# Sink probabilities divided before their transposes, and a reordered start and end, in a two-layer encoder trunk

## The chip, the cores and the metric

The kernel runs on one core of one Trainium2 chip. The metric is the device time of one execution in microseconds (us); lower is better. A core has five engines that run their own instruction streams and wait for each other by semaphores: TensorE (PE, matmuls; PEld is its weight load), VectorE (DVE), ScalarE (ACT), GpSimd (POOL) and SyncE (SP). SP, ACT and POOL also issue DMA transfers.

## The reference

Input is `x` of 256 tokens by 1024 columns, all in float32. Two layers follow; each is

```
x = x + 1/2 * SwiGLU_1(RMSNorm(x))                  # 1024 -> 2816 -> 1024
h = RMSNorm(x)
[qA kA vA qB kB vB] = h @ W_in
oA = windowed attention, 8 query heads on 2 key heads, 64 wide, ALiBi, one sink logit a head
oB = differential attention, 4 heads: softmax1 - lambda * softmax2, then RMSNorm per head
x = x + concat(oA, oB) @ W_out
x = x + 1/2 * SwiGLU_2(RMSNorm(x))
```

and a last RMSNorm gives the output. Of the windowed attention the part that matters here is

```python
m = jnp.maximum(jnp.max(scores, axis=-1, keepdims=True), sink_l)
e = jnp.exp(scores - m)
p = e / (jnp.sum(e, axis=-1, keepdims=True) + jnp.exp(sink_l - m))
out = jnp.einsum('bnkgqj,bnjkd->bnqkgd', p.astype(v.dtype), vb)
```

The sink logit takes part in the denominator only.

## The kernel before

**Precision.** Nearly every product is made from three fp32r products. Each operand is split into a high part (a rounding cast to fp32r) and a low part (the value less the high part); the product is high·high + low·high + high·low. For weights, ACT makes the high part and DVE the low part; `emit_split` (line 207) does both for half of one weight load.

**Weights and their order.** All weights stream once from HBM in loads of up to 1 MB (`specs`, one `Step` each). Six raw buffers hold loads that have landed. `ahead(n)` (line 244) emits, as far as half-load number `n`, the next splits, and with each buffer that comes free the next DMA on SP. How far it goes at each point of the program comes from the table `LEAD` (line 32): an entry is a number of half loads ahead of the load then in use; "start" and "open0" serve the first feed-forward block, "first0", "mid0" and "last0" its later groups, "mix" the attention stage, "close" the end of a block. ACT and DVE run their instructions in the order that comes out of this, so an entry decides what stands in front of what on these engines. PE is kept in program order everywhere. In the attention stage, between lines 1035 and 1157, `kept[0]` is False: there a planner orders the instructions of ACT, DVE and POOL by a timeline of its own, and `urgent()` raises the priority of what is made inside it.

**The feed-forward groups.** Groups 2 to 4 of the first feed-forward block of layer 0, and 1 to 4 of the others, are computed by a scheme of seven products in the place of eight (`by_sevens`, line 743), which adds some weight blocks by accumulating DMAs from POOL and some by DVE.

**The start.** `x` is fetched in quarters of 256 columns: the first by ACT's queue, the others by SP's, between the first pieces of the weights (line 473 on). `grow1`, the first norm's gain, is turned into columns by PE. `keep_busy` runs fp32 matmuls of the identity with itself. Then `take_x(0)` transposes two blocks of x on PE (`Norm.turn`), makes the operand's high part on ACT and its low part on DVE (`Norm.operands`), and the splits of the first gate and up weights are interleaved with that. `first_chunk` (line 603) holds the first six real matmuls. The squares for the norm run on ACT, and the norm's factor `r` is applied after the matmuls.

**The norm's factors in the attention stage.** `Norm.spread` (line 457) makes a 128x256 block with each token's factor down a column: DVE multiplies the identity by the factors (`dg`), one fp32 matmul with a block of ones spreads them.

**The attention stage** (`mix`, line 959). Heads of the windowed attention come in four chunks of two heads. `soft_a` (line 1023) makes a chunk: PE's scores, DVE's bias and minimum, ACT's exponential with its sums, then the sink's exponential `es`, added to the denominators `den_a`. It returns the exponentials not divided. `soft_b` does the same for differential attention. `keys_first_a` and `keys_first_b` transpose the probabilities, eight PE transposes and two copies out of PSUM each. While these run, PE makes the value projection of B (`vsl`). The division of A comes at the end: `ra` is the reciprocal of all denominators, POOL spreads it to a block `rw` of the output's layout, `turn_sums` transposes that with four PE transposes for each pair `cp` of chunks and copies it to `rT`, and DVE multiplies the attention output by it before `split`. The products of B with its values (`osl`) stand between the transposes and these.

**The end.** The last down projection is arranged so that the first 128 tokens finish early; `close` adds and squares, `finish(t)` scales 128 rows by the norm's factor, the left 512 columns on ACT and the right 512 on DVE, and stores each half with one DMA (ACT's queue and SP's).

Of the kernel before, what the change touches and what calls it, by code (L numbers as in the profile page):

```python
# [46 lines left out]
def trunk(ctx: ExitStack, tc: tile.TileContext, x, n1, g1, u1, d1, nm, w_in, sink,  # L47
# [159 lines left out]
    def emit_split(i, j):  # L207
# [132 lines left out]
    class Norm:  # L340
# [14 lines left out]
        def turn(self, j):  # L355
            sl = halves(bank())
            for i in range(2):
# [4 lines left out]
        def operands(self, j, sl, between=None):  # L362
            xs = blk()
            self.xs.append(xs)
            gs = [gcol[:, self.g0 + 2 * j + i:self.g0 + 2 * j + i + 1] for i in range(2)]

            def high(i):
                act.activation(xs[:, i, 0:S], sl[:, i], AF.Identity, scale=gs[i])

            def low(i):  # L370
# [3 lines left out]
            if between is None:  # L374
                high(0)
                high(1)
                low(0)
                low(1)
            else:
                high(0)  # L380
                low(0)
                between()
                high(1)
                low(1)
            self.turned.append((j, sl, gs))
# [87 lines left out]
    def fetch_x(q, j):  # L473
        q.dma_start(xk[:, :, j * 256:(j + 1) * 256], x[0].rearrange("(t p) d -> p t d", p=P)[:, :, j * 256:(j + 1) * 256])
# [9 lines left out]
    for j in (2, 3):  # L484
        fetch_x(sp, j)
# [3 lines left out]
    def keep_busy(n):  # L489
        for _ in range(n):  # L490
            pe.matmul(warm[:, 0:P], lhsT=ident, rhs=ident, start=True, stop=True)

    ones = const.tile([P, P], F32, name="ones")
    pool.memset(ones, 1.0)
# [5 lines left out]
    keep_busy(4)  # L500
    pe.transpose(gsl[:, 0:16], grow1, ident[:16, :16])
    keep_busy(1)
# [100 lines left out]
    def first_chunk(accs, xs, w):  # L603
# [3 lines left out]
        for n, (i, rhs) in enumerate(((0, hi), (0, lo), (1, hi))):  # L607
# [77 lines left out]
    def ffn(norm, aside=None, before=None, final=False, sevens=SEVEN[1]):  # L685
# [152 lines left out]
        for k in (0, 2):  # L838
# [3 lines left out]
            if before is take_x:  # L842
                for step, (kk, i) in enumerate(((k, 0), (k, 1), (k + 1, 0), (k + 1, 1))):
                    if step or k:
                        tokens((gs, us)[i], norm.xs, ws[i], 0, (kk,))
                    else:
                        first_chunk(gs, norm.xs, ws[0])
                    if step == 1:
# [110 lines left out]
    def mix(l, norm, nxt_norm):  # L959
# [63 lines left out]
        def soft_a(c, q):  # L1023
# [6 lines left out]
            dve.tensor_tensor(den, den, es, op=ALU.add)  # L1030
            return e
# [42 lines left out]
        for k0 in (0, 4):  # L1074
            w = weights()
            for k in range(4):
# [28 lines left out]
        ra = tmp("ra", 1, (P, 4, 4))  # L1105
# [192 lines left out]
```

## Time and profile before

| | |
|---|---|
| median of 3 runs | 911.79 us (911.65 to 912.84) |
| the profiled execution | 912.2 us |
| its span, first to last instruction | 910.4 us |
| busy PE / DVE / ACT / POOL | 902.3 / 777.5 / 613.8 / 64.9 us |
| moved by DMA | 200.83 MB |

The span lies inside the profiled execution's time; 1.8 us are around it. A line of the timeline gives the start in us from the span's start, the duration, the engine, the line of the kernel (here nearly always that of the helper on line 62, so tiles tell more), the operation, out<-in by tile names, the shapes and the count; in brackets stands the idle time ahead of it and what ended that. `ps` and `xy` are PSUM tiles, `s` the large work tiles (operands, exponentials, probabilities), `w` a split weight, `raw` a landed load, `q` and `v` the operands of the seven products. SPq, ACTq and POOLq are DMA issues. A line of the groups gives busy time and mean ns of one, then idle time ahead. A line of the waits gives us in total, how often, and the longest.

### The profile page before, as it was taken

What the parts mean: (1) busy time and instruction counts of PE and PEld (TensorE: products, weight loads), DVE (VectorE), ACT (ScalarE), POOL (GpSimd) and SP (SyncE); (2) the same over time, 40 slices, a digit from 0 to 9 for tenths busy, and PEclk for the clock granted to TensorE, in tenths of its full rate; (3) what the DMA queues carried; (4) which work ended last, traced back from release to release, by engine and by line L of the source; (5) the groups of instructions that cost most, each with busy time, mean ns of one, the idle gap of its engine ahead of it and who ended that gap; (6) DMA issues with size and microseconds to landing.
All of it is one profiled execution on the core that took longest, in us unless ns stands there. A gap on an engine that the chain in (4) does not pass through costs nothing.

```text
span 910.4 us, 12060 instructions
## 1 busy us (share of the span) xinstructions
PE 902.3 (99%) x4486; PEld 754.2 (83%) x4486; DVE 777.5 (85%) x1053; ACT 613.8 (67%) x975; POOL 64.9 (7%) x83
## 2 busy tenths in 40 slices
PE   9999999999999999999999999999999999999997
PEld 8888888888888888888888888888888888888886
DVE  5859999879876899999778999997896878999894
ACT  6856677677776766677575776676766686776660
POOL 0411000000001001000000101000001000101011
PEclk9999999999999999999999999999999999999999
DMA  9998897956048788897966898897720786898731
GB/s 331 336 271 235 232 317 249 266 141 224 1 145 236 176 269 247 239 306 249 304 186 163 254 282 265 238 303 214 219 98 1 256 215 176 235 311 250 222 114 47
DMA packets 114060, 200.83 MB, mean 221 GB/s; under 512 B 3663, under 2 KB 31377, under 8 KB 114001
## 3 DMA queue, kind: packets, MB, share of 16 engines
q1 hardware_dynamic: 97344, 167.53, 54.1%
q0 software_dynamic: 16096, 31.75, 20.1%
q8 instruction: 35, 0.57, 0.3%
q10 hardware_dynamic: 560, 0.79, 0.3%
q14 instruction: 25, 0.20, 0.1%
HBM read 199.00 MB, written 1.05 MB: 220 GB/s over the span
## 4 chain that ended last, share of the span: by engine, by line
PE 91%; DMA 5%; DVE 1%; ACT 1%; issue 1%; POOL 0%; SPq 0%; POOLq 0%; ACTq 0%
PE ps L62 69%; PE xy L62 22%; DMA raw<-in_ffn_w_up_dram 4%; DVE w L62 1%; DMA raw<-in_ffn_w_gate_dram 1%; ACT w L62 1%; ACT junk L62 0%; POOL r L62 0%; ACT s L62 0%; DVE s L62 0%; ACT tmp L62 0%; SPq L172 0%; DVE xk L62 0%; DVE q L62 0%; POOLq L1293 0%
## 5 line engine op out<-in xcount | busy, mean ns | idle before, releaser
L62 DVE TENSOR_TENSOR w<-raw,w 128x1024 fp32r<-128x1024 f32 (+1 forms) x458 | 476.7, 1099 | 36.1 <-ACT w L62 35.1
L62 PE MATMUL ps<-w,s 128*128 128x512 f32 (+1 forms) x2046 | 473.7, 389 | 0.3 <-DVE s L62 0.3
L62 ACT CAST w<-raw 128x1024 fp32r<-128x1024 f32 (+1 forms) x458 | 405.0, 953 | 60.6 <-DVE raw L62 40.9
L62 PEld LDWEIGHTS ps<-w,s 128*128 128x128 f32 x2046 | 380.2, 188 | 78.7 <-ACT tmp L62 0.8
L62 PE MATMUL xy<-w,s 128*128 128x512 f32 x528 | 125.7, 391 | 0.0
L62 PEld LDWEIGHTS xy<-w,s 128*128 128x128 f32 x528 | 98.3, 188 | 20.3
L62 PE MATMUL xy<-w,q 128*128 128x512 f32 x360 | 88.1, 393 | 0.0
L62 PEld LDWEIGHTS xy<-w,q 128*128 128x128 f32 x360 | 66.5, 188 | 13.2
L62 PE MATMUL ps<-s,w 128*128 128x512 f32 (+1 forms) x384 | 70.2, 339 | 0.0
L62 POOL DMA_DIRECT2D raw<-in_ffn_w_up_dram x30 | 38.9, 1315 | 432.6 <-DVE w L62 262.6
L62 DVE TENSOR_TENSOR raw<-raw,raw 128x2048 f32<-128x2048 f32 x30 | 68.7, 2289 | 0.5
L62 PEld LDWEIGHTS ps<-s,w 128*128 128x128 f32 x384 | 58.9, 188 | 8.4
L62 ACT ACTIVATE s<-ps,gcol 128x256 fp32r<-128x256 f32 (+1 forms) x80 | 31.4, 478 | 38.3 <-PE ps L62 38.3
L62 PE MATMUL ps<-w,q 128*128 128x512 f32 x180 | 43.2, 389 | 0.0
L62 PE MATMUL ps<-w,v 128*128 128x512 f32 x180 | 43.2, 389 | 0.0
L62 ACT CAST s<-ps 128x512 fp32r<-128x512 f32 x32 | 18.1, 593 | 36.5 <-PE ps L62 36.3
L62 PEld LDWEIGHTS ps<-w,q 128*128 128x128 f32 x180 | 33.8, 188 | 7.0
L62 PEld LDWEIGHTS ps<-w,v 128*128 128x128 f32 x180 | 33.8, 188 | 7.0
L62 DVE TENSOR_TENSOR s<-ps,s 128x512 fp32r<-128x512 f32 x32 | 21.3, 688 | 18.0 <-ACT s L62 17.9
L62 ACT ACTIVATE s<-s,negm 128x256 f32<-128x256 f32 x64 | 31.7, 498 | 6.1 <-DVE negm L62 6.0
L62 PE MATMUL ps<-ident,s 128*128 128x128 f32 x256 | 34.0, 273 | 0.0
L62 PEld LDWEIGHTS ps<-ident,s 128*128 128x128 f32 x256 | 29.7, 140 | 4.8 <-issue 0.8
(128 smaller groups left out, 557.2 us busy)
## 6 DMA issues: line engine op xcount, KB each, us to landing
raw<-in_ffn_w_down_dram SPq DMA_DIRECT2D x44, 1024.0 KB, 7.3
raw<-in_ffn_w_gate_dram SPq DMA_DIRECT2D x39, 1024.0 KB, 7.4
raw<-in_ffn_w_up_dram SPq DMA_DIRECT2D x39, 1024.0 KB, 7.1
raw<-in_ffn_w_up_dram POOLq DMA_DIRECT2D x30, 1024.0 KB, 9.8
raw<-in_w_in_dram SPq DMA_DIRECT2D x14, 1024.0 KB, 7.7
raw<-in_ffn_w_gate_dram SPq DMA_DIRECT2D x8, 512.0 KB, 8.0
raw<-in_ffn_w_up_dram SPq DMA_DIRECT2D x8, 512.0 KB, 9.0
raw<-in_w_in_dram SPq DMA_DIRECT2D x8, 512.0 KB, 6.8
```

The costliest lines, as they stand in the source:

```text
L62: ins = issue(*a, **k)
```

## The change

1. `soft_a` divides each chunk's exponentials by the denominators at once: a reciprocal and a broadcast product on DVE. `ra`, `rw`, `turn_sums` and the product by `rT` go; `split` reads the attention output from PSUM. The order of the transposes changes: `keys_first_b(1)` comes after the value projection, `keys_first_a(2)` and `(3)` after the `osl` products; the scaling of `vB` is made urgent.
2. The first 256 columns of x come as two eighths, on ACT's queue and on SP's; `take_x` turns and splits them one after the other; DVE instead of ACT casts the very first weight piece; `first_chunk` takes its second and third products in the other order. `keep_busy` multiplies a tile `wake` that DVE sets, and has six calls in the place of seven.
3. `spread` gives the factors in a high and a low part by two fp32r matmuls.
4. The last 128 rows are scaled and stored in column quarters, by four DMAs.
5. Entries of `LEAD` change.

```diff
-LEAD = dict(start=(5, 7, 10, 10),
-            open0=(2, 0, 0, 2, 6, 6, 8, 6, 5, 6, 1, 10, 2, 5, 7, 7, 8, 0),
-            first=(1, 1, 1, 7, 12, 15, 16, 19, 19, 22, 22),
+LEAD = dict(start=(2, 7, 8, 6),
+            open0=(2, 0, 0, 2, 3, 6, 8, 6, 5, 6, 1, 10, 1, 5, 7, 6, 8, 0),
+            first=(1, 1, 2, 8, 12, 15, 16, 19, 19, 22, 22),
...
-            mid0=(6, 9, 12, 14, 15, 15, 19, 19, 19, 22, 24),
-            last0=(2, 8, 12, 13, 15, 15, 19, 20, 20, 23, 25),
-            first0=(2, 3, 3, 4, 7, 11, 11, 14, 14, 18, 18),
-            open=(8, 12, 11, 9, 11, 11, 9, 5),
-            close0=(7, 5, 7, 5, 6, 10, 3, 10, 5, 11, 4, 7, 1),
-            close=(1, 8, 9, 9, 6, 8, 8, 9, 1, 7, 5, 4, 6),
-            mix=(10, 2, 0, 2, 9, 2, 3, 5, 6, 11, 5, 2, 3, 1, 6, 5, 2, 4, 1, 6, 7, 8, 6, 11, 7, 8))
+            mid0=(4, 9, 12, 15, 15, 15, 19, 19, 19, 22, 24),
+            last0=(2, 8, 12, 13, 15, 15, 19, 20, 20, 22, 25),
+            first0=(0, 0, 3, 6, 6, 11, 11, 11, 12, 18, 18),
+            open=(10, 11, 9, 7, 11, 11, 9, 5),
+            close0=(6, 3, 7, 5, 6, 10, 3, 10, 5, 11, 4, 6, 1),
+            close=(0, 8, 9, 9, 6, 2, 7, 6, 1, 10, 5, 4, 8),
+            mix=(10, 0, 0, 0, 11, 3, 2, 6, 8, 9, 5, 1, 3, 0, 3, 5, 2, 2, 4, 5, 4, 8, 1, 10, 4, 9))
@@ emit_split
-            act.copy(h_, r_)
+            if i + j + a:
+                act.copy(h_, r_)
+            else:
+                dve.tensor_copy(h_, r_)
+                yield
@@ spread
-            dg = tmp("dg", 1, (P, S))
+            dg = tmp(dt=F32R)
             for t in range(2):
-                dve.tensor_scalar_mul(dg[:, t * P:(t + 1) * P], ident, self.r[:, t:t + 1])
-            pe.matmul(sl[:, 0:S], lhsT=ones, rhs=dg, start=True, stop=True)
+                c, r = slice(t * P, (t + 1) * P), self.r[:, t:t + 1]
+                dve.tensor_scalar_mul(dg[:, 0, c], ident, r)
+                dve.scalar_tensor_tensor(dg[:, 1, c], in0=ident, scalar=r, in1=f(dg[:, 0, c]), op0=ALU.mult, op1=ALU.subtract)
+            for i in range(2):
+                pe.matmul(sl[:, 0:S], lhsT=ones, rhs=dg[:, i], start=i == 0, stop=i == 1)
@@ the start
-    fetch_x(act, 0)
+    fetch_x(act, 0, P)
+    wake = const.tile([P, P], F32, name="wake")
+    dve.memset(wake, 1.0)
...
+        if j == 0:
+            fetch_x(sp, P, P)
         if j == 1:
-            fetch_x(sp, 1)
+            fetch_x(sp, 256)
@@ take_x
         if k == 0:
-            sl = norm.turn(0)
-            keep_busy(2)
+            norm.sl = norm.turn(0, (0,))
+            keep_busy(1)
             next(g)
-            norm.operands(0, sl, lambda: next(u))
+            norm.operands(0, norm.sl, (0,))
+            next(g)
+            next(u)
+        elif k == 0.25:
+            norm.operands(0, norm.turn(0, (1,), norm.sl), (1,))
             next(g)
             next(u)
@@ soft_a
             dve.tensor_tensor(den, den, es, op=ALU.add)
+            dve.reciprocal(es, den)
+            ev = e.rearrange("p t (a n) -> p (t a) n", a=2)
+            dve.tensor_tensor(ev, ev, es.unsqueeze(2).to_broadcast([P, 4, 256]), op=ALU.mult)
             return e
@@ mix
-                    aT.append(keys_first_b(1))
+        with urgent():
+            act.activation(vB[:, 0], vsl[0], AF.Copy, scale=norm.r[:, 0:1])
+            dve.tensor_scalar_mul(vB[:, 1], vsl[1], norm.r[:, 1:2])
+        aT.append(keys_first_b(1))
         pT = [keys_first_a(0)]
-        act.activation(vB[:, 0], vsl[0], AF.Copy, scale=norm.r[:, 0:1])
-        dve.tensor_scalar_mul(vB[:, 1], vsl[1], norm.r[:, 1:2])
-        for c in range(1, 4):
-            pT.append(keys_first_a(c))
+        pT.append(keys_first_a(1))
...
+        for c in (2, 3):
+            pT.append(keys_first_a(c))
@@ the products with the values
-            rT = turn_sums(cp)
...
-            dve.tensor_tensor(t_, oa[cp], rT, op=ALU.mult)
-            split(oT[cp], t_)
+            split(oT[cp], oa[cp])
@@ finish
-        act.mul(ob[:, 0], xk[:, t, 0:512], rf)
-        dve.scalar_tensor_tensor(ob[:, 1], in0=xk[:, t, 512:D], scalar=rf, in1=gf[0][:, 1], op0=ALU.mult, op1=ALU.mult)
-        for j, q in enumerate((act, sp)):
-            q.dma_start(out[0, t * P:(t + 1) * P, j * 512:(j + 1) * 512], ob[:, j])
+        for c in ((0, 512),) if t == 0 else ((0, 256), (256, 512)):
+            a, b = [slice(j * 512 + c[0], j * 512 + c[1]) for j in range(2)]
+            oa, og = ob[:, 0, c[0]:c[1]], ob[:, 1, c[0]:c[1]]
+            act.mul(oa, xk[:, t, a], rf)
+            dve.scalar_tensor_tensor(og, in0=xk[:, t, b], scalar=rf, in1=gf[0][:, 1, c[0]:c[1]], op0=ALU.mult, op1=ALU.mult)
+            sp.dma_start(out[0, t * P:(t + 1) * P, b], og)
+            (sp if t and c[0] == 0 else act).dma_start(out[0, t * P:(t + 1) * P, a], oa)
```

More of the change, by code (lines that the diff above doesn't have):

```diff
@@ L353, in pair, with turn @@
             self.operands(j, self.turn(j))
-        def turn(self, j):
-            sl = halves(bank())
-            for i in range(2):
+        def turn(self, j, of=range(2), sl=None):
+            sl = halves(bank()) if sl is None else sl
+            for i in of:
                 for t in range(2):
@@ L360, in turn, with operands @@
             return sl
-        def operands(self, j, sl, between=None):
-            xs = blk()
-            self.xs.append(xs)
+        def operands(self, j, sl, of=range(2)):
+            if 0 in of:
+                self.xs.append(blk())
+            xs = self.xs[j]
             gs = [gcol[:, self.g0 + 2 * j + i:self.g0 + 2 * j + i + 1] for i in range(2)]
-            def high(i):
+            for i in of:
                 act.activation(xs[:, i, 0:S], sl[:, i], AF.Identity, scale=gs[i])
-            def low(i):
+            for i in of:
                 dve.scalar_tensor_tensor(xs[:, i, S:512], in0=sl[:, i], scalar=gs[i], in1=f(xs[:, i, 0:S]),
                                          op0=ALU.mult, op1=ALU.subtract)
[L374 to L385, printed above, removed]
+            if 1 in of:
+                self.turned.append((j, sl, gs))
         def copies(self, n=KC // 2):
@@ L490, in keep_busy @@
         for _ in range(n):
-            pe.matmul(warm[:, 0:P], lhsT=ident, rhs=ident, start=True, stop=True)
-    ones = const.tile([P, P], F32, name="ones")
-    pool.memset(ones, 1.0)
+            pe.matmul(warm[:, 0:P], lhsT=wake, rhs=wake, start=True, stop=True)
+    ones = const.tile([P, P], F32R, name="ones")
+    pool.memset(f(ones), 1.0)
     mhalf = const.tile([P, 8], F32, name="mhalf")
@@ L847, in ffn @@
                         first_chunk(gs, norm.xs, ws[0])
+                        before(0.25)
                     if step == 1:
@@ L1102, in turned @@
             return halves(sl)
-        ra = tmp("ra", 1, (P, 4, 4))
-        dve.reciprocal(ra, den_a)
-        rw = blk(F32)
-        for t in range(2):
-            pool.tensor_copy(rw[:, t].rearrange("p (c a d) -> p c a d", c=4, a=2),
-                             ra[:, :, 2 * t:2 * t + 2].unsqueeze(3).to_broadcast([P, 4, 2, 64]))
-        def turn_sums(cp):
-            turned(rw, cp, rsl[cp])
-            rT = tmp()
-            act.copy(rT, halves(rsl[cp]))
-            return rT
         oT = [blk() for _ in range(4)]
-        rsl, both = [bank() for _ in range(2)], pair()
+        both = pair()
         osl = both
```

14 lines of the change are left out of this document (6 added, 8 removed).

## The prediction

> **What bounds the kernel now.** I read the page first, then who waited for whom on the TensorE, then stretches, then the order of time at the places that the change touches.
>
> ```profile
> span 910.4 us, 12060 instructions
> PE 902.3 (99%) x4486; PEld 754.2 (83%) x4486; DVE 777.5 (85%) x1053; ACT 613.8 (67%) x975; POOL 64.9 (7%) x83
> ```
> ```profile
> PE ps L62 <- DVE s L62: 0.3, 1, 0.3
> ```
> ```profile
> 25.00:50.00 25.00, 25.00 (x116) 20.81 (x115) 22.09 (x25) 20.16 (x30) 11.57 (x31) 1.00 1.04 339
> 70.00:190.00 120.00, 120.00 (x556) 99.82 (x556) 112.69 (x124) 82.21 (x111) 5.14 (x4) 1.00 0.89 259
> 239.40:246.20 6.80, 6.80 (x52) 5.79 (x52) 4.77 (x24) 5.19 (x21) 0.00 (x0) 1.00 0.01 2
> 246.20:253.20 7.00, 7.00 (x65) 7.00 (x64) 4.23 (x7) 3.16 (x6) 1.16 (x2) 1.00 0.00 1
> ```
>
> The third fence gives a stretch in us from the span's start and its length, then the busy time of PE, weight loads, DVE, ACT and POOL, the granted TensorE clock, the DMA share and GB/s. PE (TensorE) is busy 99% of the span, its clock is granted in full (1.00 in each stretch), and behind its first matmul its list of waits has one entry, 0.3 us. A modelled busy time can hide stalls, so I also looked at the distances between matmul starts. So the time is: when the first real matmul starts, plus the PE work, plus what follows the last matmul. An edit can gain only where it removes PE work, starts it sooner or shortens the tail; anything on DVE (VectorE) or ACT (ScalarE) gains nothing by itself and loses where PE comes to wait. DVE is the next bound, 112.69 of 120 us in the stretch from 70 to 190. The DMA engines are full early (share 1.04 from 25 to 50).
>
> **The change, part by part.**
>
> *Sink division.* Each mixing stage now turns a spread-out block of reciprocals with eight PE transposes (`turn_sums`, four for each `cp`). They go, with POOL's spreading copies, two ACT copies, two DVE products and the reciprocal `ra`.
>
> ```profile
> 239.35 0.26 DVE L62 TENSOR_TENSOR den_a<-den_a,es 128x4 f32<-128x4 f32 x2 [1.18 <-ACT es L62]
> 240.50 0.48 DVE L62 CUSTOM_DVE_ANT_0 s<-ps,distA,nsnk 128x256 f32<-128x256 f32 x1 [0.89 <-PE ps L62]
> 245.46 0.28 ACT L62 ACTIVATE es<-es 128x4 f32<-128x4 f32 x2
> 246.16 3.65 PE L62 MATMUL ps<-ident,s 128*128 128x128 f32 x32
> 249.65 3.74 PE L62 MATMUL xy<-v,s 128*128 128x128 f32 x32
> 253.22 0.60 PE L62 MATMUL ps<-ident,s 128*128 128x128 f32 x4
> 253.75 1.95 PE L62 MATMUL ps<-s,vA 128*64 128x256 f32 x16
> 255.63 0.66 PE L62 MATMUL ps<-ident,s 128*128 128x128 f32 x4
> 256.22 1.95 PE L62 MATMUL ps<-s,vA 128*64 128x256 f32 x16
> ```
> ```profile
> 253.39 31.29 PE ps L62 x164
> 700.53 31.29 PE ps L62 x164
> ```
>
> From start to start the two groups hold PE for 253.75 - 253.22 = 0.53 and 256.22 - 255.63 = 0.59 us: 1.12 us a layer. The chain has the same piece of 31.29 us in both layers, so 2 x 1.12 = **-2.2 us**. That is on the path, since PE is. The transposes of the probabilities stay, only in another order (`keys_first_b(1)` later, `keys_first_a(2)` and `(3)` behind the 32 `osl` matmuls).
>
> What comes in is on DVE: for each of four chunks a reciprocal and a 128x1024 product whose second operand is a broadcast.
>
> ```profile
> L62 DVE TENSOR_TENSOR w<-raw,w 128x1024 fp32r<-128x1024 f32 x354 | 411.6, 1220 | 31.0 <-ACT w L62 30.1
> L62 DVE COPY s<-ps 128x512 f32<-128x512 f32 x12 | 8.3, 689 | 1.3 <-PE ps L62 1.1
> L62 DVE SCALAR_TENSOR_TENSOR s<-s,rc 128x256 f32<-128x256 f32 x16 | 7.0, 479 | 0.1
> L62 DVE RECIPROCAL rc<-den_b 128x2 f32<-128x2 f32 x8 | 1.3, 159 | 0.6 <-ACT s L62 0.6
> L62 DVE CAST distA<-dist_i 128x512 f32<-128x512 int32 x1 | 0.4, 417 | 0.0
> ```
>
> No such broadcast product is in the trace. A subtraction of that size took 1.220 us; I take that (four of the 256-wide form would be 4 x 0.479 = 1.9, the upper end; two of the 512-wide cast 0.8, the lower). So 4 x (1.22 + 0.16) = 5.5 us a layer, ahead of the transposes. From 239.4 to 253.2 DVE is idle 13.8 - 4.77 - 4.23 = 4.8 us. It nearly fits. Followed through: the first two products can run from 239.9, when their sums are there (239.35 + 0.26, two reciprocals; DVE idled until 240.50), to about 242.4. The other two need sums whose `es` was made at 245.46; the scores ahead of them now wait 1.9 us for DVE (242.4 instead of 240.5), so these products end near 251. PE transposes at (249.65 - 246.16) / 32 = 0.109 us. The eight of `keys_first_b(1)` are gone from their earlier place, so it comes to 246.16 - 0.87, does 24 there (2.62), then `osl` (253.22 - 249.65 = 3.57), and wants chunk 2 at 251.5 and chunk 3 at 252.4. A lucky order makes the wait 0, a copy or two (0.69) in front of the last product about 1 us a layer. I take 0.25: **+0.5 us** in all. Waiting behind these products on DVE stand PSUM copies of the transposes (0.69 each) and `vB`, which the change marks urgent; they have that same slack. The later `split(oT, oa)` reads PSUM directly: shorter, and hidden behind the output projection.
>
> *Spread in two parts.* One fp32 matmul becomes two fp32r ones of 256 columns.
>
> ```profile
> 193.52 1.55 PE L62 MATMUL xy<-s,w 128*128 128x512 f32 x8
> 197.68 0.59 PE L62 MATMUL ps<-dg,ones 128*128 128x256 f32 x2
> 197.92 0.93 PE L62 MATMUL ps<-s,w 128*128 128x512 f32 x3
> ```
>
> The old one appears as two instructions and the next starts 197.92 - 197.68 = 0.24 us later, which looks like no gain. But the three after it (512, 256 and 512 wide) take 0.93, where the eight of the row above (four of each width) take 1.55, so (1.55 - 0.28) / 7 = 0.18 a matmul, and three should take 0.35 + 0.39 = 0.74. The 0.19 us missing belongs to the old spread: 0.43. Two fp32r matmuls of 256 columns cost about 0.23. So -0.2 twice, **-0.4 us**. (The Trainium skill, "FP8 and Floating Point Precision", section TensorE Precision Notes, says true fp32 takes four passes through the array. The 0.43 agrees with four passes better than the 0.24 does; by the bare 0.24 this term would be 0.) Its two more DVE instructions (under 0.48 each) lie between 193.8 and 195.8, where DVE waits for PE.
>
> *First eighth of x, DVE cast, earlier warm-up, the new order.*
>
> ```profile
> 3.07 0.49 SPq L474 DMA_DIRECT2D xk<-in_x_dram  x1
> 4.49 0.62 ACT L62 CAST w<-raw 128x512 fp32r<-128x512 f32 x1 [1.77 <-DMA raw<-in_ffn_w_gate_dram]
> 5.27 0.47 ACT L62 ACTIVATE s<-ps,gcol 128x256 fp32r<-128x256 f32 x1 [0.16 <-PE ps L62]
> 5.79 1.83 PE L62 MATMUL ps<-w,s 128*128 128x512 f32 x6
> 8.83 0.60 PE L62 MATMUL ps<-ident,xk 128*128 128x128 f32 x4
> ```
> ```profile
> xk<-in_x_dram SPq DMA_DIRECT2D x1, 256.0 KB, 5.3
> ```
>
> Today ACT casts the weights from 4.49 and only then makes the operand (5.27 + 0.47), so PE starts at 5.79. With the cast on DVE (0.42 to 0.69, by the rows above) both can be ready at 5.0 to 5.2: 0.6 to 0.8 us sooner. But PE next needs the second quarter of x, which lands at 3.07 + 5.3 = 8.4 and is transposed at 8.83; sooner than 8.4 to 8.6 it cannot go on. One more DMA on SP ahead of it (0.49 of issue) moves no bytes ahead, yet could push it by 0.5. So -0.4 to 0; I take **-0.2 us**. `wake` only lets `keep_busy` begin before the identity is there; whatever it speeds up in the first matmuls ends at the same landing, so it adds 0.
>
> *The planner's lists.* At 69 us stands the only stall of the body:
>
> ```profile
> 65.66 3.49 DVE L62 TENSOR_TENSOR w<-raw,w 128x1024 fp32r<-128x1024 f32 x3
> 69.07 0.68 DVE L62 TENSOR_TENSOR s<-ps,s 128x512 fp32r<-128x512 f32 x1
> 69.16 0.39 PE L62 MATMUL ps<-w,s 128*128 128x512 f32 x1
> 69.81 2.56 PE L62 MATMUL ps<-w,s 128*128 128x512 f32 x10 [0.26 <-DVE s L62]
> ```
>
> 69.81 - 69.16 = 0.65 between starts where 2.56 - 0.39 over nine steps gives 0.24: 0.4 us lost, because `turn_one`'s subtraction stands behind three weight subtractions. The new `first0` begins (0, 0, 3) instead of (2, 3, 3): fewer weights ahead of it. That takes **-0.4 us** if the weights themselves still come in time. In the opening the lists ask for less ahead (start 2 instead of 5):
>
> ```profile
> 17.65 1.14 ACT L62 CAST w<-raw 128x512 fp32r<-128x512 f32 x2
> 18.41 5.60 PE L62 MATMUL ps<-w,s 128*128 128x512 f32 x24
> ```
>
> This cast moves behind the squares, to end near 21.2, and PE wants it half way through the 24 matmuls, at 18.41 + 2.7 = 21.1: a tie. What the other changed entries do can't be read off; each moves half a load, one DVE subtraction of 1.22 us, and I put them at 0: nothing below (no other stall is there to remove), and some single subtractions, 1 to 5 us, above.
>
> *Last rows in four DMAs.*
>
> ```profile
> 905.60 0.75 DVE L62 SCALAR_TENSOR_TENSOR s<-xk,rf,s 128x512 f32<-128x512 f32 x1 [0.67 <-POOL rf L62]
> 906.36 0.36 ACTq L62 DMA_DIRECT2D out_dram<-s  x1
> ```
>
> Halves are ready at 905.60 + 0.48 = 906.1 and 906.5, but SP issues three of the four, 0.36 each: 906.1, 906.4, 906.8. The last is issued 0.4 us later than now and carries half the bytes, worth 128 KB at 339 GB/s = 0.4. I take **0**, between -0.4 and +0.4. (The Trainium skill, "DMA: Bandwidth & Descriptors", section Anatomy of one DMA, gives about 2.0 us fixed and the rest by bytes: as an estimate from that page half the bytes land 0.3 us sooner, and the term would be +0.1. No run here shows a transfer of that half size.)
>
> **Sum.** -2.2 + 0.5 - 0.4 - 0.2 - 0.4 + 0 = -2.7 us. The profiled execution took 912.2 (span 910.4 and 1.8 around it), 0.4 above the median of the runs, 911.79. So 909.5 on its scale and 909.1 on the median's.
>
> **The rivals.**
> *The gains are eaten (no change).* The wait for chunks 2 and 3 is 0.9 us a layer and the tie at 21.1 us is lost by 0.3: 909.1 + 2 x 0.65 + 0.3 = 910.7. For it: DVE is short by 5.5 - 4.8 = 0.7 us. Against: that counts idle time after 239.4 alone, and work that goes (`ra`, the products) frees more behind.
> *VectorE becomes the bound of the mixing stage (slower).* If all four products run only after the last sums (245.46 + 0.28 + 0.26 = 246.0), with four PSUM copies and `vB` (costed as a copy) between them, they end at 246.0 + 5.5 + 5 x 0.69 = 255.0, and PE waits 255.0 - 252.4 = 2.6 us a layer: 909.1 - 0.5 + 5.2 = 913.8. It cancels the gain from 1.6 us a layer on and makes it slower by 0.2% from 2.5. For it: nothing but the planner's order keeps the first two products early. Against: DVE idles when they become ready.
> *The lists starve PE (slower).* Each load late by one subtraction costs 1.2 us; four such places give 909.1 + 4.9 = 914.0. For it: DVE at 94% between 70 and 190. Against: the lists of that stretch barely change.
> *The division's PE work doesn't go.* Excluded by the code: the eight transposes are gone.
>
> **How the numbers follow.** Forecast 0.54 (909.1; its own range 907.6 to 910.0: below, no wait and each term at its lower end, -2.2 - 0.4 - 0.4 - 0.4 - 0.4 = -3.8, and the 0.4 between profiled run and median; above, the bound), gains eaten 0.24 (910.7), DVE as bound 0.14 (913.8), lists 0.08 (914.0). A measurement of this kernel tells about 0.2%, 1.8 us, from no change: faster 0.54, same 0.24, slower 0.22. The range takes 907.6 at one end and reaches to 913.2, short of the two slower cases' middle: about 0.2 is left out.
>
> **What would show it.** Right: no PE transposes between the `vA` matmuls near 250 and 700; a start to start of about 0.23 us for the `dg` pair and nothing missing behind it; first 512-wide matmul near 5.1 and the transposes after it at 8.4 to 8.6; no gap at 69; PE's waits still under 1 us. Wrong: PE waiting for DVE `s` ahead of the last eight probability transposes, or for `w` anywhere, by more than 1.5 us a layer; or the last output landing later after the last matmul than now.

## The result and the profile after

The median went from 911.79 us (911.53 to 912.84, 13 runs) to 910.16 us (909.28 to 910.88, 13 runs). The ratio is 0.998, its 95% interval 0.9972 to 0.9988: 1.6 us are gained, which the interval tells from nothing, but which lies just under the 0.2% (1.8 us) that the prediction named as the bound of a change. The forecast was 909.1. The profiled execution took 910.6, with a span of 908.8 (before: 912.2 and 910.4).

The page after, its span and busy times:

```profile
span 908.8 us, 12037 instructions
PE 900.8 (99%) x4468; PEld 753.0 (83%) x4468; DVE 785.9 (86%) x1070; ACT 610.1 (67%) x971; POOL 62.8 (7%) x79
```

PE has 18 matmul records fewer and is busy for 1.5 us less; DVE took over 8.4 us of work. PE's waits are down to one, ahead of the first `keep_busy`:

```profile
PE ps L62 <- DVE wake L62: 1.0, 1, 1.0
```

By these two views PE waits for nothing behind its first matmul, and yet only 1.6 us of 2.7 arrived. Where the rest went shows when the same PE instruction is looked up in both traces. First the start. The order of time on PE, before and then after (the first two numbers are start and duration; x gives the instructions):

```profile
4.17 1.06 PE L62 MATMUL ps<-ident,xk 128*128 128x128 f32 x4
5.02 1.06 PE L62 MATMUL ps<-ident 128*128 128x128 f32 x4
...
7.46 1.53 PE L62 MATMUL xy<-w,s 128*128 128x512 f32 x6
```
```profile
3.69 0.69 PE L62 MATMUL ps<-ident,xk 128*128 128x128 f32 x2
4.17 0.63 PE L62 MATMUL ps<-wake 128*128 128x128 f32 x2
4.95 2.93 PE L62 MATMUL ps<-w,s 128*128 128x512 f32 x6
7.67 0.63 PE L62 MATMUL ps<-ident,xk 128*128 128x128 f32 x2
7.95 2.37 PE L62 MATMUL xy<-w,s 128*128 128x512 f32 x6
10.16 0.60 PE L62 MATMUL ps<-ident,xk 128*128 128x128 f32 x4
```

The first real matmul starts at 4.95 instead of 5.79, as meant. But its group of six takes 2.93 us, where the same group took 1.83 before, and the next six 2.37 instead of 1.53. Start to start, most 512-wide matmuls are 0.426 us behind the one before them until 9.69 us, and about 0.23 us from there on; in the trace before the short distance began at 6.33. So PE runs at about half pace for 3.4 us longer, and the transposes of x's second quarter begin at 10.16 instead of 8.83 (+1.33). The granted clock of a window does not show it; the same stretch gives, before and after (columns as in the prediction's windows, PE busy first, the clock third from the end):

```profile
6.40:8.40 2.00, 2.00 (x11) 1.64 (x10) 1.79 (x4) 1.61 (x3) 0.00 (x0) 1.00 0.95 317
```
```profile
6.40:8.40 2.00, 2.00 (x7) 1.60 (x6) 0.21 (x1) 0.06 (x1) 0.00 (x0) 1.00 1.01 305
```

Both read fully busy and 1.00. The counts tell: 11 matmuls in 2 us, then 7. A slow matmul looks like a busy one. The 1.00 is an absence of records: the column takes off only the time that the trace records at a lower clock, and the trace's first clock record, which grants the full clock, begins at 6.24 us before and at 9.55 after. Ahead of it there is no record, and a window there reads 1.00 as well. So the trace does hold the moment, and it agrees with the distances.

The further rows after, at the places of the prediction's steps: the stall at 69 us, the spread, the mixing stage on PE and on DVE.

```profile
67.65 2.98 PE L62 MATMUL xy<-w,q 128*128 128x512 f32 x12
70.47 4.70 PE L62 MATMUL ps<-w,s 128*128 128x512 f32 x20
...
198.43 0.40 PE L62 MATMUL ps<-tmp,ones 128*128 128x256 f32 x2
198.67 1.55 PE L62 MATMUL ps<-s,w 128*128 128x512 f32 x8
...
245.88 2.78 PE L62 MATMUL ps<-ident,s 128*128 128x128 f32 x24
248.50 3.74 PE L62 MATMUL xy<-v,s 128*128 128x128 f32 x32
252.07 1.91 PE L62 MATMUL ps<-ident,s 128*128 128x128 f32 x16
253.91 3.67 PE L62 MATMUL ps<-s,vA 128*64 128x256 f32 x32
257.51 1.20 PE L62 MATMUL ps<-w,s 128*128 128x512 f32 x4
```
```profile
244.72 2.36 DVE L62 TENSOR_TENSOR s<-s,es 128x1024 f32<-128x1024 f32 x2
...
248.55 1.19 DVE L62 TENSOR_TENSOR s<-s,es 128x1024 f32<-128x1024 f32 x1
249.66 0.68 DVE L62 COPY s<-ps 128x512 f32<-128x512 f32 x1
250.27 1.21 DVE L62 TENSOR_TENSOR s<-s,es 128x1024 f32<-128x1024 f32 x1
```

No transposes stand between the `vA` products any more, and no PE row has a wait in brackets. The same instruction's start in both traces, in us:

| instruction | before | after | difference | won or lost since the row above |
|---|---|---|---|---|
| transposes of x's second quarter | 8.83 | 10.16 | +1.33 | the start, +1.33 |
| first `xy<-w,q` of the first seven products | 66.34 | 67.65 | +1.31 | |
| the same, a group later | 97.71 | 98.46 | +0.75 | the stall at 69 us, -0.56 |
| first output projection | 258.09 | 257.51 | -0.58 | spread -0.19, division -1.14 |
| last addition of DVE (second layer done) | 903.98 | 902.07 | -1.91 | spread -0.19, division -1.14 |
| end of the span | 910.4 | 908.8 | -1.6 | tail, +0.3 |

The body gains 3.2 us, a little more than forecast; the start gives 1.3 back. The spread's part is the distance from the first of its pair to the third start behind it, 0.66 before and 0.47 after in both layers; the division's is the rest.

### The profile page after: what moved, and what is told of

The parts are those of the page before. It is cut to its first block, busy times and chain, and to the rows that moved or that the text cites. A ratio compares the mean times of both kernels' runs of the same rounds, so it can differ in the third digit from the quotient of the medians.

```text
span 908.8 us, 12037 instructions
## 1 busy us (share of the span) xinstructions
PE 900.8 (99%) x4468; PEld 753.0 (83%) x4468; DVE 785.9 (86%) x1070; ACT 610.1 (67%) x971; POOL 62.8 (7%) x79
## 3 DMA queue, kind: packets, MB, share of 16 engines
HBM read 199.00 MB, written 1.05 MB: 220 GB/s over the span
## 4 chain that ended last, share of the span: by engine, by line
PE 99%; issue 0%; DVE 0%; ACT 0%; POOLq 0%; POOL 0%
PE ps L62 73%; PE xy L62 25%; ACT s L62 0%; DVE xk L62 0%; POOLq L1288 0%; POOL rf L62 0%; DVE w L62 0%; DVE wake L62 0%; DVE gcol L62 0%; DVE tot L62 0%; DVE tmp L62 0%
## 5 line engine op out<-in xcount | busy, mean ns | idle before, releaser
L62 DVE TENSOR_TENSOR w<-raw,w 128x1024 fp32r<-128x1024 f32 (+1 forms) x458 | 476.3, 1099 | 31.8 <-ACT w L62 30.8
L62 ACT CAST s<-ps 128x512 fp32r<-128x512 f32 x36 | 20.4, 592 | 44.7 <-PE ps L62 44.5
L62 DVE TENSOR_TENSOR s<-ps,s 128x512 fp32r<-128x512 f32 x36 | 24.1, 688 | 21.4 <-ACT s L62 21.3
L62 DVE SCALAR_TENSOR_TENSOR s<-ps,gcol,s 128x256 fp32r<-128x256 f32 x48 | 20.4, 478 | 15.2 <-ACT s L62 15.2
L62 ACT COPY ps<-ps 128x512 f32<-128x512 f32 x15 | 8.6, 570 | 34.7 <-PE ps L62 34.7
```

Source lines behind the costliest of these rows:

```text
L62: ins = issue(*a, **k)
```

## The experiments

Theory: the start loses because PE now pauses between `keep_busy` and the first real matmul, and the pause puts off the moment from which PE runs at full pace. For the pause: in the trace before, four fp32 pieces of 128 columns take 5.02 - 4.17 = 0.85 us, 0.21 each. The `keep_busy` of after is two such pieces from 4.17, done at 4.60, and the first real matmul starts at 4.95: a pause of 0.35 us that the trace before does not have. Rivals: the start's loss is chance from run to run; or it is the new order of x and of the casts; and for the smaller gain in all, that the division or the tail costs something that the table above hides.

| kernel | median us (lowest to highest, runs) | before, same chip | ratio and 95% interval |
|---|---|---|---|
| after, again (e7) | 910.32 (909.33 to 910.84, 11) | 911.84 | 0.9981, 0.9973 to 0.9990 |
| before without the `keep_busy` (e5) | 913.73 (912.30 to 914.33, 11) | 911.84 | 1.0018, 1.0010 to 1.0027 |
| before with the new start (e6) | 912.95 (912.08 to 913.50, 11) | 911.84 | 1.0010, 1.0001 to 1.0019 |
| after, pause filled (e1) | 909.57 (909.11 to 909.76, 8) | 912.21 | 0.9970, 0.9960 to 0.9981 |
| after with the old start (e2) | 908.97 (908.80 to 909.20, 5) | 912.21 | 0.9966, 0.9953 to 0.9978 |
| after with the old tail (e3) | 910.38 (909.42 to 910.92, 11) | 912.21 | 0.9978, 0.9969 to 0.9986 |
| before with the division (e4) | 909.94 (909.25 to 910.58, 10) | 912.21 | 0.9976, 0.9967 to 0.9985 |
| e1 with x's second quarter earlier (e8) | 909.43 (909.19 to 909.84, 8) | 911.84 | 0.9973, 0.9963 to 0.9983 |
| e8 with the old opening lists (e9) | 909.36 (908.65 to 910.36, 6) | 912.37 | 0.9970, 0.9958 to 0.9981 |
| e2 with the first cast on DVE (e10) | 909.22 (908.77 to 909.73, 5) | 912.37 | 0.9968, 0.9956 to 0.9981 |
| before with the new `first0` (e11) | 912.42 (911.76 to 913.52, 11) | 912.37 | 1.0001, 0.9992 to 1.0010 |

### The pause alone, put into the kernel before (e5)

```diff
             sl = norm.turn(0)
-            keep_busy(2)
             next(g)
```

> The kernel before with one thing changed: the two warm-up matmuls between the first transposes of x and the first real matmul are left out, so TensorE pauses there for about 0.8 us; no operand comes later. Theory A (a pause in the warm-up puts the rise of the clock off to about 9.5 us): first real matmul at 5.8 as before, then 0.43 us apart until about 9.5, later work 1.3 to 1.8 us later, median 913.3 to 913.7. Theory B (the rise is chance alone): median 911.8 to 912.3, and the profile shows the rise anywhere between 5.5 and 9.7.

It costs 1.9 us, though it takes work away from PE and nothing waits for that work. PE's order of time:

```profile
4.34 1.06 PE L62 MATMUL ps<-ident,xk 128*128 128x128 f32 x4
6.00 2.93 PE L62 MATMUL ps<-w,s 128*128 128x512 f32 x6 [0.59 <-ACT s L62]
8.72 1.73 PE L62 MATMUL xy<-w,s 128*128 128x512 f32 x6
10.29 0.60 PE L62 MATMUL ps<-ident,xk 128*128 128x128 f32 x4
```

The four transposes take 0.85 us (5.02 - 4.17 before), so PE pauses for 6.00 - 4.34 - 0.85 = 0.8 us. The first matmul is only 0.2 us later than before, but the six take 2.93, and full pace begins at 9.13. This is the kernel before in all else, so neither the order of x nor the casts are needed for a loss: the pause is enough. Ten of its eleven runs lie above the slowest of before on that chip (912.64 of 30), which speaks against chance.

The moment of full pace, taken as the first start that is followed at the short distance (0.23 us for 512 columns, 0.11 instead of 0.21 for the fp32 pieces of 128), and the start of the trace's first clock record were in all the traces, in us and in the order of the kernels named:

| | full pace by the distances | first clock record |
|---|---|---|
| no pause ahead of it (e9, e11, e2, e1, e8, before, e10, e4) | 4.37, 5.13, 5.15, 5.69, 5.89, 6.33, 6.99, 7.70 | 4.35, 5.10, 5.14, 5.44, 5.92, 6.24, 7.02, 7.51 |
| a pause ahead of it (e6, e7, e5, e3, after) | 7.24, 8.93, 9.13, 9.38, 9.69 | 7.22, 8.89, 9.10, 9.38, 9.55 |

The two agree within 0.3 us in all thirteen: what came late is the clock. From this record to the fall of the clock at the kernel's end there are 897.70 us in nine traces and 901.12 in four, which is 263 and 264 times 3.413 us; so the clock changes on a fixed grid of 3.41 us. PE's first matmul starts at 1.05 us in kernels with `wake` and at 1.35 in the others, so without a pause full pace came 3.3 to 6.4 us after it.

The Trainium skill, "TensorE: Matmul & The Clock Gate", section Part 1: The HAM clock gate, says that TensorE runs at half rate until it has been busy through one window of about 3.4 us, and that these windows run freely. The half rate agrees (0.426 and 0.227 us), and so do the grid and the spread: about one window to two after the first matmul, depending on the phase. A pause that spoils a window would put the rise off by one more, which fits the second row but for e6.

In e6 the window that ends with the rise begins at 3.81 and holds the same pause of 0.35 us as after, so this pause alone did not spoil a window. In after, e3 and e7 the window one earlier (from 2.72, 2.55 and 2.06), which ended without a rise, holds the pause and also the breaks around the transpose of `grow` (0.14 us ahead of it at 3.48, and the small transpose itself), which e6's does not; and e1, e8 and e9 have these breaks without the pause and rose in time. That would fit a limit on the idle time of one window, above either of the two and below both; no run was made to test it.

### The new start alone, on the kernel before (e6)

```diff
-LEAD = dict(start=(5, 7, 10, 10),
+LEAD = dict(start=(2, 7, 8, 6),
...
-    fetch_x(act, 0)
+    fetch_x(act, 0, P)
+    wake = const.tile([P, P], F32, name="wake")
...
-            sl = norm.turn(0)
-            keep_busy(2)
+            norm.sl = norm.turn(0, (0,))
+            keep_busy(1)
```

> The kernel before with the new start alone (and its two lists). From the profiles so far: the second quarter's transposes at about 10.1 in place of 8.83, later work 1.3 us later, of which the stall at 69 us swallows 0.4: median 912.6 to 913.2. As the prediction had it (-0.2): 911.6. If it is chance alone: between the two.

With the rest of the new start, the cast on DVE and the order of `first_chunk`, which the excerpt leaves out, this costs 1.1 us (0.1 to 1.7 by the interval). The profiled run was one of its two fastest (912.14), and the trace has the earliest full pace of the five with a pause:

```profile
4.95 2.69 PE L62 MATMUL ps<-w,s 128*128 128x512 f32 x6
```

Six in 2.69 us are still slow; the second quarter's transposes come at 9.08, even in this case later than the 8.83 of before.

### The old start in the kernel after (e2)

```diff
-LEAD = dict(start=(2, 7, 8, 6),
+LEAD = dict(start=(5, 7, 10, 10),
...
-    fetch_x(act, 0, P)
+    fetch_x(act, 0)
...
-            norm.sl = norm.turn(0, (0,))
-            keep_busy(1)
+            sl = norm.turn(0)
+            keep_busy(2)
```

> The changed kernel with the start of the kernel before: quarters of x, ScalarE casts the first weights, warm-up on the identity, the first two lists. If the start is where the expected gain went (transposes of the second quarter at 10.16 where it was 8.83): first real matmul at 5.8, those transposes at 8.8, all later work 1.3 us sooner, median about 908.8. If the loss lies elsewhere: 910.0 to 910.4.

The excerpt leaves out that ACT casts the first piece again and `first_chunk` has its old order. It has the lowest ratio of all, though those of e10, e1 and e9 lie within its interval: 3.2 us under before, where the change as it came has 1.5 to 1.6. PE's order of time:

```profile
5.15 0.61 PE L62 MATMUL ps<-ident 128*128 128x128 f32 x4
6.08 1.66 PE L62 MATMUL ps<-w,s 128*128 128x512 f32 x6 [0.31 <-ACT s L62]
7.57 1.53 PE L62 MATMUL xy<-w,s 128*128 128x512 f32 x6
8.94 0.60 PE L62 MATMUL ps<-ident,xk 128*128 128x128 f32 x4
```

The first matmul is 1.1 us later than in the changed kernel and the second quarter's transposes 1.2 us earlier. PE pauses here too, for 0.3 us by the wait in brackets, but behind the rise: the four fp32 pieces ahead of it take 0.61 us instead of the 1.06 of before, so they already run at full pace. The pause did not undo it. e2's whole interval lies below 0.998, the ratio of the change; its upper end, 0.9978, just reaches into the change's interval (0.9972 to 0.9988).

### The pause filled (e1)

```diff
             norm.sl = norm.turn(0, (0,))
-            keep_busy(1)
+            keep_busy(3)
             next(g)
```

> The changed kernel with three warm-up matmuls in the place of one between the first two transposes of x and the first real matmul, so that TensorE does not pause there (it paused from 4.60 to 4.94 us). Theory A (the pause keeps the clock low): the 512-wide matmuls are 0.227 us apart from about 6 us on in place of 9.7, the transposes of the second quarter of x come at 8.4 to 8.9 in place of 10.16, median about 909.0 in place of 910.16. Theory B (when the clock rises is a matter of chance from run to run, whatever TensorE did in those 0.3 us): median within 0.4 of 910.16. Theory C (late operands, not the clock): the matmuls stay 0.43 us apart, 910.2 to 910.5.

One number changed takes 1.0 us off the changed kernel by the medians (2.6 under before, against 1.6). The two intervals overlap, but the slowest of e1's eight runs (909.76) is faster than eight of the 13 of after. PE's waits and order of time:

```profile
PE ps L62 <- DMA xk<-in_x_dram: 0.4, 1, 0.4
...
4.18 1.44 PE L62 MATMUL ps<-wake 128*128 128x128 f32 x6
5.32 1.69 PE L62 MATMUL ps<-w,s 128*128 128x512 f32 x6
...
6.98 1.64 PE L62 MATMUL xy<-w,s 128*128 128x512 f32 x6
9.01 0.66 PE L62 MATMUL ps<-ident,xk 128*128 128x128 f32 x4 [0.39 <-DMA xk<-in_x_dram]
```

The first matmul comes 0.4 us later and the six take 1.69. Now PE reaches the second quarter at 8.6 and waits for it to land, at 9.0. That is the other half of the start. In the trace before the quarter's DMA was issued at 3.07 and had landed by 8.4; with one more DMA on SP ahead it goes out half a microsecond later. The DMA issues of e1 on SP (the eighth, then the quarter):

```profile
2.11 0.43 SPq L469 DMA_DIRECT2D xk<-in_x_dram  x1
...
3.58 0.43 SPq L469 DMA_DIRECT2D xk<-in_x_dram  x1
```

So the eighth of x gains nothing in this form: what it wins at the first matmul is waited away at the second quarter.

### The second quarter of x earlier, and the old lists (e8, e9)

e8 is e1 with

```diff
         if j == 0:
             fetch_x(sp, P, P)
-        if j == 1:
             fetch_x(sp, 256)
```

> The kernel of the first run (three warm-up matmuls there) with the second quarter of x issued ahead of the second pieces of the weights, since in that run TensorE waited for this quarter until 9.01 us. If the landing sets it: those transposes at 8.3 to 8.5 and all later work 0.5 to 0.7 us sooner, median about 909.0 in place of 909.57. If the second weight pieces, now later, take over as the last to arrive: no gain, 909.4 to 909.8.

The second quarter's transposes begin at 8.66, without a wait, but the time stays (0.9973; e1 0.9970). What is late next shows 10 us on, in the 24 matmuls that took 5.60 us before:

```profile
18.24 6.16 PE L62 MATMUL ps<-w,s 128*128 128x512 f32 x24
20.44 6.07 ACT L62 CAST w<-raw 128x512 fp32r<-128x512 f32 x9
```

The cast of their weights now starts at 20.44, where before it began at 17.65: the list asks for less ahead and the squares go first. PE runs into it and loses some 0.5 us between 20.8 and 21.9. In the changed kernel itself PE comes there 1.5 us later and loses nothing. e9 puts the old lists back:

```diff
-LEAD = dict(start=(2, 7, 8, 6),
-            open0=(2, 0, 0, 2, 3, 6, 8, 6, 5, 6, 1, 10, 1, 5, 7, 6, 8, 0),
+LEAD = dict(start=(5, 7, 10, 10),
+            open0=(2, 0, 0, 2, 6, 6, 8, 6, 5, 6, 1, 10, 2, 5, 7, 7, 8, 0),
```

> The run before this one of the same start (three warm-up matmuls, second quarter of x early), with the first two lists of the kernel before. There the transposes of that quarter came at 8.66, yet TensorE then lost 0.43 us between 20.8 and 21.9, waiting for a weight cast that the new start list puts behind the squares. If that list is the cause: no excess there, later work 0.4 to 0.5 us sooner, median about 909.0. If a late weight load is the cause: the same loss and 909.4.

The loss in the 24 matmuls is gone (5.60 again), but the time is the same as before that edit within the intervals. In the profiled run, the slowest of its six, a weight piece comes late instead:

```profile
8.25 0.60 PE L62 MATMUL ps<-ident,xk 128*128 128x128 f32 x4
10.10 1.91 PE L62 MATMUL ps<-w,s 128*128 128x512 f32 x6 [1.25 <-ACT w L62]
```

ACT waited there for the landing of `raw`, issued at 3.10 and landed 6.3 us later. The moved quarter of x alone does not explain that: e8 issues the same transfers in the same order and at the same times, and there this piece took 4.8. Why it was late in this one trace stays open. In each of the three traces in which PE was let go sooner, the next transfer or cast held it.

### The first cast on DVE, on the best start (e10)

```diff
-            act.copy(h_, r_)
+            (act.copy if i + j + a else dve.tensor_copy)(h_, r_)
```

> The second run's kernel (start of before, everything else of the changed kernel) with only the very first weight piece cast by VectorE. That run's TensorE waited 0.31 us for ScalarE's operand ahead of the first real matmul at 6.07. If the cast on VectorE alone serves this: first real matmul at 5.6 to 5.9, second quarter's transposes at 8.7, median about 908.7. If the landing of x or chance in the clock sets it: 909.0 or more.

No difference from e2 that can be told (0.9968 and 0.9966). The cast starts on DVE at 4.91, when the weight piece lands, and the first matmul comes at 5.97, right behind the `keep_busy`, against 6.08 in e2. That is less than the 5.6 to 5.9 that was expected, and the second quarter's transposes come later than in e2 (9.31 and 8.94), with the clock's rise at 7.02 and 5.14: the moment of the clock's rise can hide what the cast is worth.

### The division alone (e4)

```diff
             dve.tensor_tensor(den, den, es, op=ALU.add)
+            dve.reciprocal(es, den)
+            ev = e.rearrange("p t (a n) -> p (t a) n", a=2)
+            dve.tensor_tensor(ev, ev, es.unsqueeze(2).to_broadcast([P, 4, 256]), op=ALU.mult)
...
-            rT = turn_sums(cp)
...
-            split(oT[cp], t_)
+            split(oT[cp], oa[cp])
```

> The kernel before with the sink division alone moved (and the order of the transposes that goes with it), lists as before. The prediction's term: 2.2 us less of TensorE work, 0 to 1 us of waiting a layer. By the changed kernel's trace the waiting is nothing with its new lists: 911.79 - 2.3 = 909.5. If the new list of the attention stage is needed to keep VectorE free for the products: a wait of 0.5 to 1 us a layer and 910.5 to 911.5. The rival in which VectorE bounds the stage: 913 or more.

2.3 us under before, 1.4 to 3.0 by the interval, with the old lists. In the mixing stage there is no wait on PE, though the planner places the products otherwise than in the kernel after:

```profile
239.90 2.36 DVE L62 TENSOR_TENSOR s<-s,es 128x1024 f32<-128x1024 f32 x2
...
247.85 1.22 DVE L62 TENSOR_TENSOR s<-s,es 128x1024 f32<-128x1024 f32 x1
...
249.59 1.22 DVE L62 TENSOR_TENSOR s<-s,es 128x1024 f32<-128x1024 f32 x1
...
251.64 1.91 PE L62 MATMUL ps<-ident,s 128*128 128x128 f32 x16
```

Here the first two run at 239.90, as the prediction had followed them through; after, at 244.72, behind the scores. The last one ends 0.8 us before PE begins with the sixteen transposes here, and 0.6 us before it in the kernel after (252.07 - 250.27 - 1.21), and PE comes to the last chunk 0.9 us later still. Both orders fit. The old `mix` list does as well as the new one.

### The tail in two DMAs (e3)

```diff
-        for c in ((0, 512),) if t == 0 else ((0, 256), (256, 512)):
...
+        act.mul(ob[:, 0], xk[:, t, 0:512], rf)
+        dve.scalar_tensor_tensor(ob[:, 1], in0=xk[:, t, 512:D], scalar=rf, in1=gf[0][:, 1], op0=ALU.mult, op1=ALU.mult)
+        for j, q in enumerate((act, sp)):
+            q.dma_start(out[0, t * P:(t + 1) * P, j * 512:(j + 1) * 512], ob[:, j])
```

> The changed kernel with the last 128 rows scaled and stored whole, by two DMAs. From the start of the last addition on VectorE to the end of the span the two profiles have 6.45 us before and 6.73 after. If the four DMAs cost this: 6.45 again and a median near 909.9. If it is chance: 6.7 and 910.2. As the prediction had it (0 within 0.4): either.

910.38 against 910.16 to 910.32 of the changed kernel: no difference. From the last addition to the end of the span the traces with two DMAs take 6.45, 6.65, 6.72, 6.44, 6.59 and 6.54 us (before, e3, e4, e5, e6, e11), mean 6.56; those with four 6.76, 6.66, 6.20, 6.65, 6.77, 6.65 and 6.22 (after, e1, e2, e7, e8, e9, e10), mean 6.56. The +0.3 in the table of the result is the spread of one trace. The stores of before and after, with the median time from issue to landing last:

```profile
out_dram<-s SPq DMA_DIRECT2D x2, 256.0 KB, 2.8
```
```profile
out_dram<-s SPq DMA_DIRECT2D x3, 128.0 KB, 2.1
```

The last store is issued 3.06 us after the last addition begins (905.13), where before had 2.40 (906.38), and it lands 0.7 sooner: the two cancel.

### The list `first0` alone (e11)

```diff
-            first0=(2, 3, 3, 4, 7, 11, 11, 14, 14, 18, 18),
+            first0=(0, 0, 3, 6, 6, 11, 11, 11, 12, 18, 18),
```

> The kernel before with the list first0 of the changed kernel alone. By the prediction: the 0.4 us between the matmuls at 69.16 and 69.81 go, nothing else changes, median 911.4 (before 911.8). If it is another list or the later arrival of TensorE that took this stall away: 911.8 and the gap still there.

The stall shrinks, but the median does not move. DVE's and PE's order of time there:

```profile
65.33 3.49 DVE L62 TENSOR_TENSOR w<-raw,w 128x1024 fp32r<-128x1024 f32 x3
68.74 0.68 DVE L62 TENSOR_TENSOR s<-ps,s 128x512 fp32r<-128x512 f32 x1
...
66.36 2.98 PE L62 MATMUL xy<-w,q 128*128 128x512 f32 x12
69.18 3.12 PE L62 MATMUL ps<-w,s 128*128 128x512 f32 x12
```

Three weight subtractions still stand ahead of `turn_one`'s subtraction; they start 0.33 us sooner. The wait in brackets is gone, and from 66.36 to the next group PE needs 31.06 us, where before took 31.37 and the kernel after 30.81. A gain of 0.3 in the trace, less than the medians can tell. The other traces show a second thing: with the old list, e4, e5 and e6 reach this place at 67.02, 67.79 and 66.64 instead of 66.34, and take 30.8 as well. Whenever PE is 0.3 us late or more the stall is gone by itself. It was worth 0.5 us only to a PE that came on time.

### The changed kernel again (e7)

> The changed kernel once more, on this chip beside the others. Theory A: the rise of the clock again near 9.4 to 9.7 us, span 908.6 to 909.1. Theory B: anywhere from 5.5 on, so a span of 907.5 is as likely as one of 908.8. In either case a median of 909.9 to 910.5.

0.9981 after 0.998: the result stands. The second quarter's transposes come at 9.86, full pace at 8.93. The 13 runs of after fall into two groups, five at 909.28 to 909.49 and eight at 910.06 to 910.88, and the trace of none of the first group was at hand; that these reached full pace early, as e6 did, would fit and is not shown.

## Why the prediction was right and wrong

- **Sink division, -2.2 and +0.5 for waits.** The PE work went as worked out: -1.14 us a layer by the table, -2.3 by the medians of e4. The wait was 0. The product took 1211 ns (eight of them), for which a subtraction of the same size had stood at 1220. The step that failed is the charge of 0.25 us a layer: the worked path had the products end near 251, ahead of the 251.5 at which PE wants them, and they did come in time, in two orders.
- **Spread, -0.4.** Right: -0.19 in both layers. The eight matmuls behind the pair take 1.55 us, as undisturbed ones do, so the 0.19 that was missing did belong to the old fp32 matmul. The term of 0, which goes by the bare 0.24, is thereby ruled out. (The Trainium skill, "FP8 and Floating Point Precision", section TensorE Precision Notes: its four passes are borne out by the 0.43.)
- **The start, -0.2.** Wrong by 1.5 us, and the term that misses the forecast. The first matmul at 4.95 was foreseen (5.0 to 5.2), and so was that an added DMA on SP could push the second quarter by 0.5 (9.0 instead of 8.4 in e1). What failed is the sentence that whatever `wake` speeds up ends at the same landing and adds 0: `keep_busy` went from two calls to one ahead of the first matmul, the PE was left to pause, the clock rose at 9.55 us instead of 6.24, and 9 of the next 12 matmuls ran 0.2 us longer (1.8 us), with two transposes (0.28) now among them; 0.84 of that was won back by the earlier beginning. The removed `keep_busy` was not priced at all, so it stood at nothing without a reason. The landing at 8.4 then was no bound at all: PE came to it at 10.16.
- **The planner's lists, -0.4.** The stall went (-0.56), but it would have gone anyway, since PE came 1.3 us late; on its own the list gives about 0.3 in a trace, and nothing that the median shows (e11). The tie at 21.1 us is real and lost by some 0.5 us when PE is on time (e8). In the changed kernel PE's lateness hides it.
- **Tail, 0.** Right in sum, from seven traces against six, with both of its parts too small: the last store is issued 0.7 us later, not 0.4, and lands 0.7 sooner, not 0.4. The fit that the prediction took from the Trainium skill, "DMA: Bandwidth & Descriptors", section Anatomy of one DMA, is given there for transfers issued by GpSimd, and these stores are issued by SP and ACT; its 0.3 us is short of the 0.7 measured, and the measurement decides.
- **The rivals.** The time came out near "gains eaten" (910.7), but not by its mechanism: neither the wait for the last chunks nor the tie took anything. That VectorE becomes the bound and that the lists starve PE did not happen; DVE did 12.72 of 13.8 us from 239.4 on, as the window after has it, without holding PE:

```profile
239.40:253.20 13.80, 13.80 (x113) 12.50 (x112) 12.72 (x39) 9.37 (x33) 0.00 (x0) 1.00 0.26 77
```

The sum with measured terms: -2.3 (division) - 0.4 (spread) + 1.3 (start) - 0.55 (stall) + 0.3 (tail, chance) = -1.65, against 1.6 in the spans and in the medians. That the time lies within the stated range owes something to luck: the start missed by 1.5 us, and 0.5 of it was covered by a wait that did not come. The forecast's own part of the range, 907.6 to 910.0, just misses 910.16.

## What to carry to other kernels

A matmul that computes nothing can be worth more than its time: the two calls that e5 leaves out are four pieces of 0.21 us, and without them the kernel took 1.9 us more. Before one is removed or moved at the start of a kernel, ask whether PE then pauses ahead of the first real work, and look at the distances between matmul starts, since busy time and the clock column of a window show nothing of it; where the trace's own clock records can be read, their first entry tells the moment. Starting PE sooner gained nothing here, since not everything on its next ten microseconds (the next landing, the next cast) came sooner too; e1, e8 and e9 each met the next one. And a change of many parts is best undone part by part: everything but the new start and its two lists (e2) gives 3.2 us where all together give 1.6.

## What the runs showed of the hardware

- A pause of 0.35 to 0.8 us on PE ahead of its first real matmuls went with full pace at 7.2 to 9.7 us instead of 4.4 to 7.7, and cost 1.9 us where nothing else was changed (e5). The clock's first record lies at the same moments, within 0.3 us; a window ahead of it reads 1.00.
- From its rise to its fall the full clock lasted 263 or 264 times 3.413 us in all thirteen traces.
- Without a pause ahead of it the rise still differs by 3.2 us between traces (4.35 to 7.51), which is worth up to 1.5 us, as an estimate: at 0.426 instead of 0.227 us a matmul, 3.2 us at half pace is 7.5 matmuls, each 0.2 us late. Differences under 1 us in one pair of traces may be this alone; the medians of 5 to 13 runs are what counts.
- An fp32 matmul of 256 columns is recorded as two instructions; the next matmul is recorded 0.24 us after the first of them, and yet the pair holds PE for 0.43, by what is missing behind it.
- Two stores of 128 KB in the place of one of 256 KB moved the end of the kernel by 0.0 us (6.56 both, seven and six traces): 0.7 us later to issue, 0.7 sooner to land (2.1 us for 128 KB, 2.8 for 256 KB).

What stays open: how much idle time a window of the clock bears (e6 rose with a pause of 0.35 us in its window; after, e3 and e7 did not with that pause and the breaks ahead of it), why e9's weight piece landed late, and whether a start can be had that brings both x's second quarter and the weights sooner.
